# A two-layer trunk with seven-product MLPs: where the steps on the first two hidden panels stand ahead of each chunk's second matrix

## The chip, the cores and the metric

The kernel runs on one core of a Trainium2 chip. The metric is the device time of one execution in microseconds (us); the time of a kernel is the median of several runs. A profile is one execution, recorded by the hardware, with its own time.

## The reference

The input is x with 256 rows (tokens) of 2048 numbers in fp32. Two layers are applied. Each has an attention (the first a forgetting attention with its own keys and values, the second a chunked attention over shared keys and values) and then an MLP. Only the MLPs matter here:

```
def sq_relu_mlp(h, g, w1, w2):
    a = jax.nn.relu(rms_norm(h, g) @ w1)
    return (a * a) @ w2

h = h + sq_relu_mlp(h, mlp_norm_g[layer], mlp_w1[layer], mlp_w2[layer])
```

w1 is 2048 x 8192 and w2 8192 x 2048, for each of the two layers.

## The kernel before

**Products in three passes.** Each fp32 operand is split in two: a high part rounded to fp32r, made on ScalarE (line 217 for weights), and a low part, the difference, made on VectorE (line 218). A product is then three passes on TensorE: high by high (line 461), activation low by weight high (463), activation high by weight low (465). The name hi (hih for a half) is a weight's high part, lo (loh) its low part.

**Chunks, panels and pairs.** The hidden width of 8192 is worked in four chunks of 2048. A chunk takes four panels of 512 hidden columns of w1 (panels 0 to 3 of the chunk) and then four panels of 512 output columns of w2, whose input is the chunk's 2048 hidden values, that is 16 tiles of 128. Two panels make a pair (class `Pair`); a chunk is thus two pairs of the first matrix and two of the second, in this order. The 256 tokens are two blocks of 128.

**Seven products instead of eight.** For some of the 16 input tiles a pair uses a scheme of Strassen's kind: over two token blocks, two groups of tiles and two panels it takes seven block products ("forms", in the order 11, T3, T2, T1, 21, T4, 22) of sums of weights and sums of activations instead of eight. In a wide pair six of the 16 input tiles go this way, and each form has a full part (f0 to f6, tiles in two sets of two, 6 matmuls) and a half part (h0 to h6, 3 matmuls). The other ten tiles are plain products in units of two tiles (12 matmuls): a3 to a7 for the first panel of the pair, b3 to b7 for the second. In `form_products`, f0 reads the first four activation tiles of the chunk's hidden panel 0, and h0 reads tiles 4 and 5, which belong to panel 1; f1 to f3 and f6 read sums of panel 0's tiles, h1 to h3 and h6 sums of panel 1's. All pairs of w2 are wide, and all of w1 but the first of each layer.

**The order of the work** is written out by hand in `Pair.plan` (lines 131 to 142) and kept on VectorE, ScalarE, TensorE and the SP queue by `keep_order`. From the second pair of a chunk to its third pair (the first of w2) TensorE does

```
... f2 h2 b7 f3 h3 a3 f4 h4 a4 f5 h5 a5 f6 h6 a6 a7 b3 b4 | f0 h0 b5 f1 h1 b6 f2 h2 b7 ...
```

where the bar marks the start of the next pair; b5 to b7 behind it still belong to the pair before. The weight splits run ahead of the products: `fetch` and `top_up` (230 to 238) split up to three full weight tiles and one half tile ahead, and issue the loads of raw tiles from the SP queue (line 200, four buffers). The four corner tiles of a pair's forms are loaded by `bring` (line 800, SP queue), their sums made by `make` (line 810, VectorE) or by an accumulating load by `put` (line 816, POOL queue), each so many units before the pair starts (`prepare`): the corner 11 four units before, T3 three, T1 two, 21 one.

**The small steps** between the units come from a list, `fill`: after the products of each a or b unit (not after forms) `run_fill` issues the next entry. When a panel of w1 is done, `turn_hidden` (852) transposes it in 32 x 32 blocks on VectorE (line 329), and puts on the list: its store to memory (339) for the next unit, its load back with rows and columns exchanged (345) for the one after, and then the steps of `take` (828) by the numbers in `uses`, where n is the panel in the chunk, c the chunk, and a number i means the i-th a or b unit from then. The steps are: 1. ReLU on ScalarE (829); 2. square as the high part, ScalarE (834); 3. square in fp32 in place, ScalarE (836); 4. the low part, the difference, on VectorE (840); then for panels 0 and 1: 5. the sums and differences over the token blocks, four operations on VectorE (284 to 287, `sums`); 6. their high part on ScalarE (291); 7. their low part on VectorE (294). Panels 0 and 2 end with a7, panels 1 and 3 with the b7 that follows among the next pair's forms.

Of the kernel before, what the change touches and what calls it, by code (L numbers as in the profile page):

```python
# [49 lines left out]
def trunk(ctx: ExitStack, tc: tile.TileContext, xT, xr, gs, hg, bf, wgate, w_in, w_oa, w1a, w1fa, w1sa, w2fa, w2sa,  # L50
# [185 lines left out]
    def fetch(ahead=AHEAD, early=EARLY):  # L236
        top_up(ahead, early)
        return ready.popleft()[:2]
# [3 lines left out]
    def run_fill():  # L242
        if fill:
            for f in fill.popleft():
                f()
# [7 lines left out]
    def acc_pair(which=None):  # L253
        if which is None:
            which, turns[0] = turns[0], 1 - turns[0]
        if which == 2:
            return [ps_s.tile([P, 512], F32, name="s") for _ in range(2)]
        return [ps_acc.tile([P, 512], F32, name="acc", tag=f"acc{which}{b}", bufs=1) for b in range(NB)]
# [16 lines left out]
    def sums(a, fs, n=2):  # L275

        w = [wk.tile([P, 512], F32, name="sum", tag="wk") for _ in range(n)]

        def part(i):
            at = i * n * P  # L280
            v = w[at // 512][:, at % 512 : at % 512 + n * P].rearrange("p (g t) -> p g t", g=n)
            return v.rearrange("p g (i c) -> p g i c", i=4) if len(a[0][0].shape) == 4 else v

        V.tensor_tensor(part(0), a[1][0], a[1][1], op=ALU.subtract)
        V.tensor_tensor(part(1), a[0][0], part(0), op=ALU.subtract)
        V.tensor_tensor(part(2), a[1][0], a[0][0], op=ALU.subtract)
        V.tensor_tensor(part(3), a[0][1], part(1), op=ALU.subtract)
        hi, lo = ([fs[k][:, i * 512 : (i + 1) * 512] for i in range(n)] for k in range(2))
        yield
        for i in range(n):  # L290
            S.activation(hi[i], w[i], AF.Copy)
        yield
        for i in range(n):
            V.tensor_tensor(lo[i], w[i], hi[i].bitcast(F32), op=ALU.subtract)
        yield
# [21 lines left out]
    def steps(make):  # L317
        box = []

        def step():  # L320
            if not box:
                box.append(make())
            next(box[0])
        return step

    def blocks32(src, z, b):
        n = src.shape[1] // P
        nb = z.shape[1] // (n * P)
        V.transpose(z.rearrange("p (j n b c) -> p b n j c", j=4, n=n, b=nb)[:, b],
                    src.rearrange("p (n j c) -> p n j c", n=n, j=4))  # L330

    def carry(z, dst, wait=1):
        w = z.shape[1]
        n = w // 4
        box = []

        def rows():
            box.append(dram.tile([P, w], F32, name="turn", tag=f"turn{w}", bufs=4))
            SY.dma_start(box[0], z)

        def columns():
            s = box[0].rearrange("(i a) f -> a i f", i=4)
            d = dst.rearrange("p (i f) -> p i f", i=4)
            for j in range(4):
                SY.dma_start(d[32 * j : 32 * j + 32], s[:, :, j * n : (j + 1) * n])

        return [[rows]] + [[]] * wait + [[columns], [], []]

    def turned(name=None):
        z = qkv.tile([P, GH * T], F32, name="z")  # L350
        return (z, qkv.tile([P, GH * T], F32, name=name, tag=name, bufs=2)) if name else z
# [310 lines left out]
    def add_fill(items):  # L662
        for i, it in enumerate(items):
            if i < len(fill):
                fill[i] = fill[i] + it
            else:
                fill.append(it)
# [155 lines left out]
    def mlp(plan, x, Sx, st, last):  # L823
        base = turns[0]
        hids = [[] for _ in range(NCH)]
        Sh = [[] for _ in range(NCH)]

        def take(t, c, n):
            S.activation(t, t, AF.Relu)
            y = acts.tile([P, 2, GH, T], F32R, name="act")  # L830
            hi, lo = (y[:, i].rearrange("p k (b i c) -> p (k b) i c", b=NB, i=4) for i in range(2))
            t3 = t.rearrange("p (i kb c) -> p kb i c", i=4, c=32)
            yield
            S.activation(hi, t3, AF.Square)
            yield
            S.activation(t, t, AF.Square)
            yield

            def low():
                V.tensor_tensor(lo, t3, hi.bitcast(F32), op=ALU.subtract)  # L840

            hids[c].extend(y[:, :, j, :] for j in range(GH))
            low()
            yield
            if n == 0:
                r = prob.tile([P, 9 * 3 * P], F32R, name="Sh", tag="p", bufs=1)
                Sh[c].extend(r[:, i : i + n] for i, n in ((0, UN), (UN, UN), (2 * UN, 512), (2 * UN + 512, 512)))
                yield from sums([[t3[:, 2 * j + b :: 4] for j in range(2)] for b in range(NB)], Sh[c])
            elif n == 1:
                yield from sums([[t3[:, 2 * j + b : 2 * j + b + 1] for j in range(2)] for b in range(NB)], Sh[c][2:], 1)  # L850

        def turn_hidden(c, n):
            zt = []

            def f(b, ps):
                if b == 0:
                    zt.extend(turned("q"))
                blocks32(ps, zt[0], b)
                if b == NB - 1:
                    step = steps(lambda: take(zt[1], c, n))  # L860
                    uses = ((4, 5, 7, 8, 9, 10, 11), (4, 5, 6, 7, 7, 8, 8), (4, 5, 6, 7), (4, 5, 5, 5))[n]
                    if not c and n < 2:
                        uses = (4, 5, 6, 7, 7, 8, 8) if n else (4, 4, 5, 6, 7, 8, 9)
                    add_fill(carry(*zt, 0)[:2] + [[step] * uses.count(i) for i in range(3, uses[-1] + 1)])
            return f

        pairs = [p for p, q, u in plan if (q, u) == (2, 0)]

        def open_pair(p):
            m = pairs.index(p)  # L870
            c, second, r = m // 4, m % 4 >= 2, m % 2
            p.x, p.fs = (hids[c], Sh[c]) if second else (x, Sx)
            p.ps = [acc_pair(base), acc_pair(2 if p.third else 1 - base)]
            if second:
                p.evac = [(last if c == NCH - 1 else residual)(2 * r + q, st.r2) for q in range(2)]
            else:
                p.evac = [turn_hidden(c, 2 * r + q) for q in range(2)]

        starts = [i for i, it in enumerate(plan) if it[1:] == (2, 0)]
        for i, (p, q, u) in enumerate(plan):  # L880
            hi, lo = ready.popleft()[:2] if q > 1 and ready else fetch()
            if p.ps is None:
                open_pair(p)
            f, kind, k = plan[i - 1]
            done = k if i and kind > 1 and kind == 2 + f.wide else None
            if q > 1:
                form_products(p.ps, hi, lo, p.x, p.fs, u, q == 3, 1 + p.wide)
                if u == 1 and q == 2 + p.wide:
                    p.t["P7"] = wk.tile([P, 512], F32, name="p7", tag="wk")
                    S.activation(p.t["P7"], p.ps[1][0], AF.Copy)  # L890
                elif u == 2 and q == 2 + p.wide:
                    V.scalar_tensor_tensor(p.ps[0][1], p.ps[1][0], -1.0, p.t["P7"], op0=ALU.mult, op1=ALU.subtract)
                if q == 2 + p.wide:
                    top_up(AHEAD - 1)
                    if u == 1:
                        S.activation(p.ps[1][0], p.ps[1][1], AF.Copy, scale=-1.0)
            else:
                products(p.ps[q], hi, lo, p.x, u, not units and not ready, p.fast)
                if p.fast and (q, u) == (0, p.own):
                    V.tensor_tensor(p.ps[1][1], p.ps[1][0], p.t["P7"], op=ALU.add)  # L900
                run_fill()
                if u == KT // UA - 1:
                    for b in range(NB):
                        p.evac[q](b, p.ps[q][b])
                nxt = next((j for j in starts if j > i), None)
                if nxt is not None:
                    d = sum(1 for it in plan[i:nxt] if it[1] < 2)
                    prepare(plan[nxt][0], d)
            if done == 1 and not f.wide:
                make(f, "T4")  # L910
            elif done == 2:
                S.activation(f.ps[0][0], f.ps[1][1], AF.Copy)
# [144 lines left out]
```

## Time and profile before

| | |
|---|---|
| time, median of 3 runs | 2114.97 us (2114.54 to 2116.11) |
| time of the profiled execution | 2118.57 us |
| its span, first to last instruction | 2116.8 us |
| mean granted TensorE clock | 0.998 of full speed |
| busy, share of the span | TensorE weight loads 82%, VectorE 76%, ScalarE 59%, GpSimd 5% |
| moved by DMA | 538.85 MB, 255 GB/s in the mean |

The rows of the profile name an engine (PE is TensorE's products, PEld its weight loads, DVE VectorE, ACT ScalarE, POOL GpSimd, SPq the DMA issues of the SP queue), a line of the kernel, the operation, what is written and read, sizes and counts. In a timeline a row begins with its start and duration in us and ends, in brackets, with the idle time before it and what ended that. Ends of matmuls are modelled, so their rows overlap a little; start to start is the safer measure. In a list of waits the three numbers are the total in us, the times, and the longest.

### The profile page before, as it was taken

Reading aid. Unit: us, or ns where it says so; the run is one execution under the profiler, and the core shown is the slowest. Engines: PE = TensorE matmul, PEld = TensorE weight load, DVE = VectorE, ACT = ScalarE, POOL = GpSimd, SP = SyncE. Lnnn points to the kernel's source line nnn. Section 1 sums busy time; section 2 is a strip of 40 time slices with the busy share of each in tenths; the row PEclk is TensorE's granted clock in tenths of the full one; section 3 lists DMA queues with packets and bytes.
Section 4 is the critical chain, followed back from the end, with each engine's and each line's share of the span. In section 5 each row is a group of like instructions: output and inputs, shape, how many; then the busy total and the mean of one; then the engine's idle time right before and its main releaser. Section 6 shows DMA issues by size and latency. Waiting matters only on the chain.

```text
span 2116.8 us, 26314 instructions
## 1 busy us (share of the span) xinstructions
PE 2091.2 (99%) x9242; PEld 1727.1 (82%) x9242; DVE 1615.5 (76%) x1944; ACT 1247.8 (59%) x1623; POOL 109.9 (5%) x123
## 2 busy tenths in 40 slices
PE   9999999999999999999999999999999999999999
PEld 8888888878878887887888888888788788788877
DVE  5767666888788778778777677678877887888786
ACT  6544445676566566566675454456665665665664
POOL 1101000000000000000001010000000000000000
PEclk9999999999999999999999999999999999999999
DMA  7787788798797799789778777788888987987885
GB/s 282 245 258 241 232 248 262 259 267 267 249 285 241 249 288 274 215 277 283 229 237 263 233 233 234 237 273 261 273 254 251 278 265 238 282 258 244 276 270 169
DMA packets 181206, 538.85 MB, mean 255 GB/s; under 512 B 36800, under 2 KB 72016, under 8 KB 181072
## 3 DMA queue, kind: packets, MB, share of 16 engines
q1 hardware_dynamic: 171248, 484.69, 68.4%
q0 software_dynamic: 9824, 52.46, 13.5%
q8 instruction: 73, 1.20, 0.2%
q14 instruction: 61, 0.50, 0.1%
HBM read 497.20 MB, written 39.87 MB: 254 GB/s over the span
## 4 chain that ended last, share of the span: by engine, by line
PE 94%; DMA 3%; DVE 2%; issue 0%; SPq 0%; ACT 0%; DVEq 0%; ACTq 0%
PE acc L463 25%; PE acc L461 25%; PE acc L465 24%; PE s L463 6%; PE s L465 6%; PE s L461 6%; DVE lo L218 1%; DMA w<-in_w2fa 1%; PE s L604 1%; PE po L634 1%; DMA q<-turn 1%; DMA raw<-in_w2sb 0%; DMA w<-in_w2fb 0%; PE s L603 0%; PE po L635 0%
## 5 line engine op out<-in xcount | busy, mean ns | idle before, releaser
L218 DVE TENSOR_TENSOR lo<-raw,hi 128x1024 fp32r<-128x1024 f32 (+1 forms) x582 | 705.0, 1215 | 235.5 <-ACT hi L217 222.1
L217 ACT ACTIVATE hi<-raw 128x1024 fp32r<-128x1024 f32 (+1 forms) x582 | 611.5, 1052 | 288.3 <-PE acc L463 214.7
L461 PE MATMUL acc<-hi,act 128*128 128x512 f32 x2122 | 586.5, 395 | 0.7 <-ACT hi L217 0.5
L463 PE MATMUL acc<-hi,act 128*128 128x512 f32 x2122 | 578.2, 391 | 0.0
L465 PE MATMUL acc<-lo,act 128*128 128x512 f32 x2122 | 575.8, 390 | 0.0
L463 PEld LDWEIGHTS acc<-hi,act 128*128 128x128 f32 x2122 | 399.5, 189 | 86.6 <-DVE act L840 2.8
L465 PEld LDWEIGHTS acc<-lo,act 128*128 128x128 f32 x2122 | 399.4, 188 | 83.5
L461 PEld LDWEIGHTS acc<-hi,act 128*128 128x128 f32 x2122 | 397.5, 188 | 82.1 <-ACT hi L217 0.8
L217 ACT ACTIVATE hi<-w 128x1024 fp32r<-128x1024 f32 x130 | 137.3, 1056 | 97.4 <-DMA w<-in_w1fa 24.0
L218 DVE TENSOR_TENSOR lo<-w,hi 128x1024 fp32r<-128x1024 f32 x130 | 157.8, 1214 | 33.7 <-ACT hi L217 33.5
L218 DVE TENSOR_TENSOR lo<-wT,hi 128x1024 fp32r<-128x1024 f32 x94 | 114.6, 1219 | 75.4 <-ACT hi L217 74.2
L217 ACT ACTIVATE hih<-w 128x512 fp32r<-128x512 f32 x120 | 75.2, 627 | 74.3 <-PE acc L463 63.3
L217 ACT ACTIVATE hi<-wT 128x1024 fp32r<-128x1024 f32 x94 | 99.1, 1055 | 31.8 <-PE acc L463 17.5
L217 ACT ACTIVATE hih<-wT 128x512 fp32r<-128x512 f32 x90 | 56.5, 628 | 95.7 <-PE acc L463 63.3
L461 PE MATMUL s<-hi,act 128*128 128x512 f32 x392 | 106.2, 389 | 0.0
L463 PE MATMUL s<-hi,act 128*128 128x512 f32 x392 | 106.1, 389 | 0.0
L465 PE MATMUL s<-lo,act 128*128 128x512 f32 x392 | 106.1, 389 | 0.0
L218 DVE TENSOR_TENSOR loh<-w,hih 128x512 fp32r<-128x512 f32 x120 | 82.3, 686 | 22.0 <-ACT hih L217 22.0
L463 PEld LDWEIGHTS s<-hi,act 128*128 128x128 f32 x392 | 73.6, 188 | 15.3
L465 PEld LDWEIGHTS s<-lo,act 128*128 128x128 f32 x392 | 73.6, 188 | 15.3
L461 PEld LDWEIGHTS s<-hi,act 128*128 128x128 f32 x392 | 73.5, 188 | 15.2
L218 DVE TENSOR_TENSOR loh<-wT,hih 128x512 fp32r<-128x512 f32 x90 | 61.9, 688 | 19.4 <-ACT hih L217 19.4
(213 smaller groups left out, 1902.8 us busy)
## 6 DMA issues: line engine op xcount, KB each, us to landing
raw<-in_w_in SPq DMA_DIRECT2D x96, 512.0 KB, 4.6
raw<-in_w2sa SPq DMA_DIRECT2D x80, 512.0 KB, 5.7
raw<-in_w2sb SPq DMA_DIRECT2D x80, 512.0 KB, 5.6
raw<-in_w1sa SPq DMA_DIRECT2D x70, 512.0 KB, 6.0
raw<-in_w1sb SPq DMA_DIRECT2D x70, 512.0 KB, 6.0
raw<-in_w_kv SPq DMA_DIRECT2D x64, 512.0 KB, 4.5
turn<-z SPq DMA_DIRECT2D x60, 512.0 KB, 4.8
w<-in_w2fa SPq DMA_DIRECT2D x32, 768.0 KB, 7.3
```

The costliest lines, as they stand in the source:

```text
L217: S.activation(hi[:, c], raw[:, c], AF.Copy)
L218: V.tensor_tensor(lo[:, c], raw[:, c], hi[:, c].bitcast(F32), op=ALU.subtract)
L461: TE.matmul(ps[:, cols], xh, cut(hi, j), start=first, stop=False, **kw)
L463: TE.matmul(ps[:, cols], xl, cut(hi, j), start=False, stop=False, **kw)
L465: TE.matmul(ps[:, cols], xh, cut(lo, j), start=False, stop=last, **kw)
L604: TE.matmul(s[:, P : 3 * P], q[:, a, P:T], k[:, a], start=True, stop=True)
L634: TE.matmul(po[:, :T], v[:, 0, a * P : (a + 1) * P], pT[:, :2], start=True, stop=False)
```

## The change

Only the numbers of `uses` for panels 0 and 1 are changed; those of panels 2 and 3 stay.

```
-                    uses = ((4, 5, 7, 8, 9, 10, 11), (4, 5, 6, 7, 7, 8, 8), (4, 5, 6, 7), (4, 5, 5, 5))[n]
+                    uses = ((4, 5, 6, 7, 8, 9, 10), (4, 4, 5, 6, 6, 7, 7), (4, 5, 6, 7), (4, 5, 5, 5))[n]
                     if not c and n < 2:
-                        uses = (4, 5, 6, 7, 7, 8, 8) if n else (4, 4, 5, 6, 7, 8, 9)
+                        uses = (4, 4, 5, 6, 6, 7, 7) if n else (4, 4, 5, 5, 6, 7, 8)
```

The units after which the steps are issued, before and after (b3 and b4 ahead of the bar, b5 behind it, that is after f0 and h0):

| step | panel 0 before | after | panel 1 before | after |
|---|---|---|---|---|
| 1 ReLU | b6 | b6 | a6 | a6 |
| 2 high part | b7 | b7 | a7 | a6 |
| 3 square | a4 | a3 | b3 | a7 |
| 4 low part | a5 | a4 | b4 | b3 |
| 5 sums | a6 | a5 | b4 | b3 |
| 6 sums' high part | a7 | a6 | b5 | b4 |
| 7 sums' low part | b3 | a7 | b5 | b4 |

In the first chunk of a layer, whose first pair has another order, panel 0's ReLU and high part both come after a3 and its square after a4, before and after the change; the other entries hold there too. In one unit's entry panel 0's steps are issued ahead of panel 1's, and all of them ahead of the transposes of a panel that ends with the unit (panel 2 at a7). The splits of weights that a unit fetches are issued ahead of its entry: at a6 that of b3, at a7 that of b4, at b3 that of f0, at b4 those of h0 and b5, after h0 that of f1, at b5 those of h1 and b6.

## The prediction, made before the changed kernel was run

> **What bounds the kernel now.** I read the page first, then the waits of the matmul engine, then a table of stretches, and last the timelines of one chunk engine by engine.
>
> ```profile
> PE 2091.2 (99%) x9242; PEld 1727.1 (82%) x9242; DVE 1615.5 (76%) x1944; ACT 1247.8 (59%) x1623; POOL 109.9 (5%) x123
> ```
>
> TensorE is busy 99% of the span, so time can only come out of places where it stands still or runs slowly. Its list of waits has two entries that matter:
>
> ```profile
> PE s L463 <- DVE act L840: 14.3, 8, 2.7
> PE s L463 <- DVE Sh L294: 5.7, 5, 1.1
> ```
>
> Both lie in the steps that the change moves. Eight times, once for each chunk in each layer, the second pass (L463) of the half product h0 of a chunk's first second-matrix pair waits for panel 1's low part (L840). Five times the second pass of the next half product, h1, waits for panel 1's sums (L294). The wait column gives 20.0 us, but not what follows a wait, so I cut out the stretch from the first matmul of f0 to the first matmul of f2 in all eight chunks. The columns are the stretch, its length, the busy time of PE, PEld, DVE, ACT and POOL, the granted clock, the DMA share and GB/s.
>
> ```profile
> 458.43:470.51 12.08, 10.16 (x44) 7.73 (x42) 9.60 (x13) 5.03 (x9) 0.00 (x0) 1.00 0.94 258
> 627.13:640.54 13.41, 11.44 (x43) 8.95 (x42) 10.73 (x15) 6.31 (x10) 0.00 (x0) 0.87 0.84 231
> 797.16:810.24 13.08, 10.11 (x44) 7.73 (x42) 10.61 (x15) 6.19 (x10) 0.00 (x0) 1.00 0.94 241
> 966.86:980.43 13.57, 10.13 (x44) 7.73 (x43) 11.10 (x15) 6.69 (x11) 0.00 (x0) 1.00 0.88 235
> 1508.35:1522.25 13.90, 11.22 (x43) 8.78 (x42) 11.44 (x16) 7.01 (x11) 0.00 (x0) 0.88 0.84 223
> 1678.87:1691.90 13.03, 10.12 (x43) 7.72 (x42) 10.56 (x14) 6.15 (x10) 0.00 (x0) 1.00 0.89 241
> 1848.52:1862.15 13.63, 11.46 (x43) 8.98 (x42) 10.94 (x15) 6.52 (x11) 0.00 (x0) 0.87 0.94 232
> 2018.76:2030.80 12.04, 10.11 (x44) 7.73 (x42) 9.56 (x13) 5.00 (x9) 0.00 (x0) 1.00 0.94 255
> 980.43:989.95 9.52, 9.52 (x44) 7.88 (x43) 9.36 (x12) 9.48 (x13) 0.86 (x1) 1.00 0.71 162
> ```
>
> The first eight rows add to 104.74 us. The ninth is the same 42 matmuls one step on (f2, h2, b7, f3, h3, a3 in place of f0, h0, b5, f1, h1, b6), without a wait: 9.52 us, or 0.227 us for a matmul. Eight times 9.52 is 76.16, so these stretches lose **28.58 us**. That is the most the change can bring. In three rows the clock is 0.87 or 0.88: 13.41 x 0.13, 13.90 x 0.12 and 13.63 x 0.13 make 5.2 us of the 28.58.
>
> **What the change moves, worked out on chunk 4 of layer one (f0 starts at 966.86).** Panel 1's low part and sums go from b4 to b3, its square from b3 to a7, its high part from a7 to a6, its sums' high and low from b5 to b4. Panel 0's steps from the square on go one unit up too. No instruction is added or removed; only places in the queues change. The waiting half product:
>
> ```profile
> 968.22 0.39 PE L461 MATMUL s<-hih,act 128*128 128x512 f32 x1
> 970.90 0.50 PE L463 MATMUL s<-hih,act 128*128 128x512 f32 x1 [2.29 <-DVE act L840]
> ```
>
> Pass one of h0 starts at 968.22, so pass two could start at 968.45 and pass three, which reads h0's own low part loh, at 968.67. Pass two started at 970.90. This is what VectorE did before it:
>
> ```profile
> 959.09 1.23 DVE L218 TENSOR_TENSOR lo<-raw,hi 128x1024 fp32r<-128x1024 f32 x1 [0.18 <-ACT hi L217]
> 961.16 1.31 DVE L329 STREAM_TRANSPOSE z<-acc 128x512 f32<-128x512 f32 x2 [0.85 <-PE acc L465]
> 962.40 1.72 DVE L810 TENSOR_TENSOR wT<-w,w 128x1536 f32<-128x1536 f32 x1
> 965.55 1.23 DVE L218 TENSOR_TENSOR lo<-w,hi 128x1024 fp32r<-128x1024 f32 x1 [1.43 <-ACT hi L217]
> 966.69 1.29 DVE L294 TENSOR_TENSOR Sh<-sum,Sh 128x512 fp32r<-128x512 f32 x2
> 967.89 0.68 DVE L218 TENSOR_TENSOR loh<-w,hih 128x512 fp32r<-128x512 f32 x1
> 968.50 1.22 DVE L218 TENSOR_TENSOR lo<-raw,hi 128x1024 fp32r<-128x1024 f32 x1
> 969.63 1.22 DVE L840 TENSOR_TENSOR act<-q,act 128x1024 fp32r<-128x1024 f32 x1
> 970.76 0.28 DVE L284 TENSOR_TENSOR sum<-q 128x128 f32<-128x128 f32 x1
> ```
>
> In order: weight low part of b4, two transposes of panel 2, the sum T3, low part of f0, panel 0's two sums' low parts, loh of h0, low part of b5, panel 1's low part L840, panel 1's sums. L840 ends at 970.85 and h0 goes on at 970.90. Afterwards the order is: b4, panel 0's L294 pair, transposes, T3, f0, L840, sums, loh, b5, panel 1's L294. So the half product will no longer wait for L840 but, in pass three, for loh, behind which L840 and the sums now stand. How late loh comes decides the gain.
>
> *ScalarE first*, since it gates the split of b4:
>
> ```profile
> 955.04 1.06 ACT L217 ACTIVATE hi<-raw 128x1024 fp32r<-128x1024 f32 x1 [0.75 <-PE acc L463]
> 956.46 1.06 ACT L829 ACTIVATE q<-q 128x1024 f32<-128x1024 f32 x1 [0.35 <-DMA q<-turn]
> 957.99 1.06 ACT L217 ACTIVATE hi<-raw 128x1024 fp32r<-128x1024 f32 x1 [0.47 <-PE acc L463]
> 958.96 1.13 ACT L291 ACTIVATE Sh<-sum 128x512 fp32r<-128x512 f32 x2
> 960.00 1.04 ACT L834 ACTIVATE act<-q 128x1024 fp32r<-128x1024 f32 x1
> ```
>
> At a6 it now does after b3's high part (955.04, next start 0.97 later) panel 0's L291 pair (1.04 from start to start), L829 (whose data landed at 956.46) and panel 1's L834, about 1.0 each, and then b4's high part: 955.04 + 0.97 + 1.04 + 2.0 = 959.05 instead of 957.99. TensorE needs b4 one unit, 12 x 0.227 us, before f0, at 964.14, which covers the 1.06 us. VectorE's split of b4 follows 1.10 later, at 960.15 (1.14 to the next), the L294 pair at 961.29 (1.20), the transposes at 962.49 (1.24), T3 at 963.73 (1.72), and VectorE is free for f0 at 965.45.
>
> *Whether f0 is there* depends on its load, w<-in_w2fa, which the ScalarE and SP queues show:
>
> ```profile
> 964.45 1.06 ACT L217 ACTIVATE hi<-w 128x1024 fp32r<-128x1024 f32 x1 [3.41 <-DMA w<-in_w2fa]
> ```
>
> ```profile
> 954.06 2.60 SPq L200 DMA_DIRECT2D raw<-in_w1sa  x2
> 956.71 0.42 SPq L800 DMA_DIRECT2D w<-in_w2fa  x1
> ```
>
> The load of form "11" is issued at 956.71, right behind the second of two raw loads, and that one waits for a raw buffer, which the weight low part of a7 on VectorE frees. Ahead of that split stand now panel 0's four sums instead of its low part:
>
> ```profile
> 953.95 1.22 DVE L840 TENSOR_TENSOR act<-q,act 128x1024 fp32r<-128x1024 f32 x1
> 955.08 2.36 DVE L218 TENSOR_TENSOR lo<-raw,hi 128x1024 fp32r<-128x1024 f32 x2
> 957.36 0.42 DVE L284 TENSOR_TENSOR sum<-q 128x256 f32<-128x256 f32 x1
> ```
>
> The sums took 957.36 to 958.91 (959.09 less the 0.18 of idle time), 1.55 us; L840 takes 1.13. The split slips by 0.42 and the load with it. f0's high part starts at 964.87, its low part 1.10 later (964.45 to 965.55 before), at 965.97, a little after VectorE is free.
>
> *Then* L840 at +1.14, sums at +2.27, loh at +3.20 (970.76 and the next row give 0.94 for the sums), done 0.68 later; with 0.05 for the semaphore pass three starts 3.94 after f0's low part, at 969.91:
>
> ```profile
> 971.70 1.22 DVE L218 TENSOR_TENSOR lo<-wT,hi 128x1024 fp32r<-128x1024 f32 x1
> ```
>
> That is 1.24 us after 968.67, where the stretch lost 4.05. **The second gap goes:** h1 starts at 974.2 with f1 and b5 in between. VectorE then does b5 (969.78), panel 1's L294 (970.9), f1 (971.5), loh of h1 (972.6, done at 973.3); h1 wants its sums at 974.4 and its loh at 974.7; f1 wants its low part, done at 972.7, at 973.8. Margins are 1.0 us or more, so I cost it at nothing; without them it would be the 1.1 us of the old wait.
>
> *The other chunks* differ only in when "11" lands. The latest and earliest of the eight rows:
>
> ```profile
> 1506.32 1.06 ACT L217 ACTIVATE hi<-w 128x1024 fp32r<-128x1024 f32 x1 [3.79 <-DMA w<-in_w2fb]
> ```
>
> ```profile
> 2014.62 1.06 ACT L217 ACTIVATE hi<-w 128x1024 fp32r<-128x1024 f32 x1 [1.68 <-DMA w<-in_w2fb]
> ```
>
> With 1.52 added, f0's low part starts 0.51 before f0 in the one and would start 2.62 before in the other; there VectorE's own chain rules (965.45 is 1.41 before 966.86). The gap is that start plus 3.94 less 1.81: 1.62 us at most, 0.72 at least. By the same sum the eight gaps are 0.72, 0.91, 0.77, 1.24, 1.62, 0.72, 1.12 and 0.72, together 7.8 us. The slow clock goes with the long gaps: the two shortest stretches, 12.08 and 12.04, have 1.00.
>
> *What I cost at nothing.* Panel 0's low part at a4 and its square at a3: between them and a5 lie T4's products and a whole unit of TensorE work; if that cover were gone, up to 1.13 us would be added to the slip of the load in each chunk. SP: the store of the transposed panel 2 waits for the transposes, 1.33 us later (961.16 to 962.49), and behind it in the queue stand a raw load for a unit beyond f3, the four column loads and the load of "21", which f4 is first to use. The tightest reader is panel 2's ReLU:
>
> ```profile
> 966.89 2.60 SPq L345 DMA_DIRECT2D q<-turn  x4
> ```
>
> ```profile
> 981.29 1.05 ACT L829 ACTIVATE q<-q 128x1024 f32<-128x1024 f32 x1
> ```
>
> Issue ends at 969.49, the reader starts 11.8 us later. The change takes 1.33 and the 2.8 gained by TensorE from that and leaves 7.7, as long as the six times larger load "11" takes from 956.71 to its reader at 964.45. POOL: the accumulating load of T1 waits for T3 and slips by 1.3 as well; its form is split for f3 only, whose products follow those of f2 (980.43 less the 2.8 gained).
>
> **The sum.** 28.6 less 7.8 is 20.8 us. The profiled execution took 2118.57 us by its own time, so 2097.8 in its terms. It was 3.6 us above the median of the three timed runs, and 2114.97 less 20.8 is **2094.2 us**.
>
> **One rule weighed.** The Trainium skill, page "TensorE: Matmul & The Clock Gate", section "What's actually happening", says that the array falls to half its clock after at least one idle activity window of about 3.4 us, on a window that does not start with the kernel. Here no wait is that long (the longest in the waits view is 2.7 us), and yet three stretches show 0.87 or 0.88: the trace does not agree with the figure. By that rule alone the slow clock would have another cause and stay, which is the second rival.
>
> **The rivals.**
> 1. *VectorE slips further.* Its chain from b4 to loh is 9.7 us of work in order with one late start (ScalarE's 959.05). If L291, L829 or L834 wait, everything behind slips, and the gap grows one for one: 1 us in each chunk makes 8 us, a gain of 12.8, 2102.2 us. Against it: L829's data was there at 956.46, and the sums that L291 reads end at 955.5, before 956.01.
> 2. *The slow clock stays* in three chunks, as it would if the gaps were not its cause: 5.2 us less gain, 2099.4. Against it: 1.00 in the ninth row and in the short ones.
> 3. *Nothing left to wait for:* loh comes in time, 28.6 us, 2086.4. It would need VectorE 0.7 to 1.6 us faster than its rows.
> 4. *No change:* the place in the list is changed but the wait is only renamed, loh taking the place of L840. This needs f0's low part 2.6 us later on average than worked out (20.8 / 8).
> 5. *Slower:* the load of "11". Every us by which its issue slips behind 957.1 moves f0's high part, and in-order VectorE with it, one for one in eight places. It decides from a slip of 0.42 + (20.8 + 4.2) / 8 = 3.5 us on; at 4.5 us the kernel takes 2114.97 + 4.2 + 8 x 1.0, about 2127. The rows give only 0.42 and at worst 1.13 more.
>
> **How the numbers follow.** About 0.2%, 4.2 us, is what a measurement of this kernel can tell from no change. The forecast gets 0.70, rival 1 0.10, rival 2 0.07, rival 3 0.03, rival 4 0.06, rival 5 0.04. Faster: the first four, 0.90; same 0.06; slower 0.04. The range runs from rival 3's 2086.4 to 2102, where each gap is twice what I work out or rival 1 has its 1 us; it takes in rival 2 and leaves out half of rival 1 and the last two, some 0.15, and a little of the forecast.
>
> **What would show it.** In the changed profile: no wait of h0 for L840 and none of h1 for L294; eight waits for loh (L218) at L465 of 0.7 to 1.6 us; the eight stretches at 10.2 to 11.2 us with the clock at 1.00; the transposes 1.3 us later; b4's high part 1 us later; the load of "11" 0.4 us later. Wrong it would be if h0 waits for more than 2 us, or if a wait for DMA appears at panel 2's ReLU.

## The result and the profile after

The changed kernel takes **2096.22 us** (median of 4 runs, 2095.46 to 2097.20), the kernel before beside it 2115.39 us (4 runs, 2114.54 to 2116.11). The ratio is 0.991, with a 95% interval of 0.9893 to 0.9927: 19.2 us faster, where 20.8 were forecast and 2094.2 us was the predicted time.

The profiled execution of the changed kernel took 2095.46 us, with a span of 2093.7 us. First, as before, the busy times of the page, and the top of the matmul engine's list of waits:

```profile
PE 2084.1 (100%) x9242; PEld 1722.6 (82%) x9242; DVE 1614.2 (77%) x1944; ACT 1247.8 (60%) x1623; POOL 110.0 (5%) x123
```

```profile
PE s L465 <- DVE loh L218: 3.9, 8, 0.5
```

The waits for L840 (14.3 us) and L294 (5.7 us) are gone from the list. One name is new, the one forecast: pass three (L465) of h0 waits for loh, eight times, 0.5 us each. The table of stretches from f0 to f2, in the columns of the prediction's table, and last the stretch without a wait:

```profile
457.36:467.68 10.32, 9.83 (x43) 7.80 (x42) 9.69 (x13) 5.57 (x9) 0.00 (x0) 1.00 1.01 245
624.32:634.62 10.30, 9.81 (x43) 7.81 (x42) 9.68 (x13) 5.57 (x9) 0.00 (x0) 1.00 1.01 251
791.24:801.58 10.34, 9.85 (x43) 7.80 (x42) 9.68 (x13) 5.57 (x9) 0.00 (x0) 1.00 1.01 234
958.22:968.56 10.34, 9.85 (x43) 7.80 (x42) 9.68 (x13) 5.57 (x9) 0.00 (x0) 1.00 1.01 244
1496.49:1506.81 10.32, 9.83 (x43) 7.80 (x42) 9.69 (x13) 5.57 (x9) 0.00 (x0) 1.00 1.00 201
1663.45:1673.75 10.30, 9.81 (x43) 7.80 (x42) 9.68 (x13) 5.57 (x9) 0.00 (x0) 1.00 1.01 225
1830.37:1840.72 10.35, 9.86 (x43) 7.81 (x42) 9.69 (x13) 5.57 (x9) 0.00 (x0) 1.00 1.00 219
1997.38:2007.69 10.31, 9.82 (x44) 7.80 (x42) 9.69 (x13) 5.57 (x9) 0.00 (x0) 1.00 0.99 226
968.56:978.08 9.52, 9.52 (x43) 7.88 (x42) 9.37 (x12) 9.52 (x13) 0.86 (x1) 1.00 0.97 267
```

All eight lengths lie between 10.30 and 10.35 us and the clock is 1.00 in each. They add to 82.58 us; less 8 x 9.52 this is **6.4 us lost**, against 28.6 before. The difference, 22.2 us, is nearly all of the 23.1 us between the two profiled executions. Another 1.07 us lie ahead of the first chunk, whose f0 starts at 457.36 instead of 458.43.

Chunk 4 of layer one, on TensorE:

```profile
959.58 0.39 PE L461 MATMUL s<-hih,act 128*128 128x512 f32 x1
959.80 0.39 PE L463 MATMUL s<-hih,act 128*128 128x512 f32 x1
960.68 0.50 PE L465 MATMUL s<-loh,act 128*128 128x512 f32 x1 [0.49 <-DVE loh L218]
961.02 1.11 PE L461 MATMUL acc<-hi,act 128*128 128x512 f32 x4
961.97 1.08 PE L463 MATMUL acc<-hi,act 128*128 128x512 f32 x4
```

Pass two of h0 follows pass one without a pause. Pass three could have started at 960.03 and starts at 960.68, 0.65 us late. A little more is lost right behind: this matmul and the next are 0.34 us apart where 0.227 us is the rule, and the four matmuls that follow take 0.95 us (961.02 to 961.97) where four take 0.91. That makes 0.15 us, and 0.80 us with the 0.65; the eight chunks lose 0.80 us in the mean. VectorE in the same chunk:

```profile
951.52 1.23 DVE L218 TENSOR_TENSOR lo<-raw,hi 128x1024 fp32r<-128x1024 f32 x1 [2.40 <-ACT hi L217]
952.67 1.29 DVE L294 TENSOR_TENSOR Sh<-sum,Sh 128x512 fp32r<-128x512 f32 x2
953.87 1.31 DVE L329 STREAM_TRANSPOSE z<-acc 128x512 f32<-128x512 f32 x2
955.10 1.72 DVE L810 TENSOR_TENSOR wT<-w,w 128x1536 f32<-128x1536 f32 x1
956.74 1.21 DVE L218 TENSOR_TENSOR lo<-w,hi 128x1024 fp32r<-128x1024 f32 x1
957.87 1.22 DVE L840 TENSOR_TENSOR act<-q,act 128x1024 fp32r<-128x1024 f32 x1
959.00 0.29 DVE L284 TENSOR_TENSOR sum<-q 128x128 f32<-128x128 f32 x1
...
959.94 0.68 DVE L218 TENSOR_TENSOR loh<-w,hih 128x512 fp32r<-128x512 f32 x1
960.54 1.22 DVE L218 TENSOR_TENSOR lo<-raw,hi 128x1024 fp32r<-128x1024 f32 x1
961.68 0.68 DVE L294 TENSOR_TENSOR Sh<-sum,Sh 128x512 fp32r<-128x512 f32 x1
```

This is the order that the prediction wrote down: b4, panel 0's L294 pair, the transposes, T3, f0, L840, the sums, loh, b5, panel 1's L294. From 952.67 on no row waits for anything: the low part of f0 starts as soon as VectorE is free, 1.48 us before f0 (958.22). ScalarE, and the load of form "11" on the SP queue:

```profile
949.48 1.06 ACT L834 ACTIVATE act<-q 128x1024 fp32r<-128x1024 f32 x1
950.45 1.04 ACT L217 ACTIVATE hi<-raw 128x1024 fp32r<-128x1024 f32 x1
...
953.84 1.06 ACT L217 ACTIVATE hi<-w 128x1024 fp32r<-128x1024 f32 x1 [1.40 <-DMA w<-in_w2fa]
```

```profile
945.42 2.93 SPq L200 DMA_DIRECT2D raw<-in_w1sa  x2
948.40 0.42 SPq L800 DMA_DIRECT2D w<-in_w2fa  x1
```

The high part of b4 (950.45) stands behind panel 1's L834. It starts 7.77 us before f0 (8.87 before the change) and gates VectorE's 951.52, as forecast. The load is issued 9.82 us before f0 (10.15 before the change). Its data is there at 953.84, 5.44 us after the issue; before the change the same interval was 7.74 us (956.71 to 964.45).

### The profile page after: what moved, and what is told of

It is laid out like the page before. It is cut to its first block, busy times and chain, and to the rows that moved or that the text cites. A ratio compares the mean times of both kernels' runs of the same rounds, so it can differ in the third digit from the quotient of the medians.

```text
span 2093.7 us, 26322 instructions
## 1 busy us (share of the span) xinstructions
PE 2084.1 (100%) x9242; PEld 1722.6 (82%) x9242; DVE 1614.2 (77%) x1944; ACT 1247.8 (60%) x1623; POOL 110.0 (5%) x123
## 3 DMA queue, kind: packets, MB, share of 16 engines
q0 software_dynamic: 9824, 52.46, 13.7%
## 4 chain that ended last, share of the span: by engine, by line
PE 99%; DVE 0%; DMA 0%; SPq 0%; issue 0%; ACT 0%; DVEq 0%
PE acc L463 26%; PE acc L461 26%; PE acc L465 26%; PE s L465 6%; PE s L461 6%; PE s L463 6%; PE s L604 1%; PE po L634 1%; PE s L603 0%; PE po L635 0%; DVE loh L218 0%; DMA raw<-in_w_in 0%; PE s L726 0%; DVE sum L287 0%; DVE lo L218 0%
## 5 line engine op out<-in xcount | busy, mean ns | idle before, releaser
L465 PE MATMUL acc<-lo,act 128*128 128x512 f32 x2122 | 574.5, 389 | 0.0
L465 PEld LDWEIGHTS acc<-lo,act 128*128 128x128 f32 x2122 | 398.1, 188 | 83.1
L465 PE MATMUL s<-lo,act 128*128 128x512 f32 x392 | 106.1, 389 | 0.0
L465 PEld LDWEIGHTS s<-lo,act 128*128 128x128 f32 x392 | 73.6, 188 | 15.3
```

The costliest lines, as they stand in the source:

```text
L465: TE.matmul(ps[:, cols], xh, cut(lo, j), start=False, stop=last, **kw)
```

## The experiments

All twelve profiles of this study can be read with one table. For each, the eight stretches from f0 to f2 were measured as above, and 8 x 9.52 us taken off:

| kernel | profiled execution, us | lost in the eight stretches, us | difference, us |
|---|---|---|---|
| before | 2118.57 | 28.58 | 2089.99 |
| before, again | 2113.68 | 24.46 | 2089.22 |
| before, low part twice | 2128.13 | 39.22 | 2088.91 |
| before, load sooner | 2109.21 | 20.20 | 2089.01 |
| panel 0's new places only | 2108.33 | 19.43 | 2088.90 |
| panel 1's new places only | 2097.44 | 8.57 | 2088.87 |
| after | 2095.46 | 6.42 | 2089.04 |
| after, again | 2095.64 | 6.58 | 2089.06 |
| after, low part twice | 2110.15 | 19.96 | 2090.19 |
| high part back | 2090.70 | 1.59 | 2089.11 |
| high part back, again | 2091.75 | 2.73 | 2089.02 |
| high part back, load sooner | 2090.21 | 0.32 | 2089.89 |

The last column lies within 0.3 us of 2089 in nine of the twelve. The three that stand 0.9 to 1.2 above it have their first f0 at 458.24 to 458.49 us instead of 457.2 to 457.6, so their extra lies ahead of the first chunk. But for this, what these kernels differ in is lost in the eight stretches. Theory A in the texts below is the prediction's mechanism: VectorE's order sets how soon h0's operands come, and the load of "11" adds to it where it lands late.

**One panel at a time.** The change moves the steps of two panels. The first kernel takes only panel 1's new numbers, the second only panel 0's:

```
-uses = ((4, 5, 6, 7, 8, 9, 10), (4, 4, 5, 6, 6, 7, 7), ...)[n]
+uses = ((4, 5, 7, 8, 9, 10, 11), (4, 4, 5, 6, 6, 7, 7), ...)[n]    # e1; first chunk likewise
+uses = ((4, 5, 6, 7, 8, 9, 10), (4, 5, 6, 7, 7, 8, 8), ...)[n]     # e2; first chunk likewise
```

> Only panel 1's numbers are changed, panel 0's stay as before. VectorE's order at the end is then: b4, transposes of panel 2 (old place), T3, f0, panel 0's L294 pair, L840, panel 1's sums, loh. Theory A (h0 now waits for loh, and loh comes when everything ahead of it in VectorE's order is done): the L294 pair, 1.20 us, is back between f0 and loh, so a gap is S + 3.33, with S the start of f0's low part against f0 on TensorE. If the load of form 11 takes as long as before the change (5.9 to 8.1 us from issue to reader), S goes from -2.75 to -0.93 and the eight stretches lose about 13 us, some 2103 us in all. If the load takes as long as after the change (5.4 to 6.5 us), S is -2.75 everywhere and they lose about 6 us, 2096 us. Theory B (h0 waits for panel 1's own chain only, so panel 0's steps do not matter): the same time as after the change, 2096 us, with the same wait of 0.65 us.

> Only panel 0's numbers are changed, panel 1's stay as before. L840 of panel 1 stands again behind loh and b5, and its sums' low part behind b6. Theory A: h0 waits in pass two for L840, S + 2.56, that is 0.2 us with the fast load and up to 2.0 with the slow one; h1 waits 1.1 to 1.4 us for L294 in every chunk. Loss 15 us with the fast load and 23 with the slow one: 2105 to 2113 us. Theory B: panel 0's part brings nothing, 2115 us.

Panel 1 alone: 2099.41 us (2097.01 to 2103.30), ratio to before 0.993 (0.9918 to 0.9943), 15.6 us faster. Panel 0 alone: 2108.41 us (2106.75 to 2112.97), ratio 0.9972 (0.9963 to 0.9981), 6.6 us faster. The first lies between the two times that theory A gave for it, the second inside its range; theory B's 2096 and 2115 us did not come. The matmul engine's waits, panel 1 alone and then panel 0 alone:

```profile
PE s L465 <- DVE loh L218: 5.4, 8, 1.0
```

```profile
PE s L463 <- DVE Sh L294: 7.9, 7, 1.1
PE s L463 <- DVE act L840: 5.5, 4, 2.6
```

Panel 1's move does the main part: it turns the waits for L840 and L294 into the wait for loh. Panel 0's move leaves both, but takes its own L294 pair off VectorE ahead of L840, so that only four waits for L840 are left. In the first kernel the wait is not the same in each chunk. Its stretches lose from 0.65 to 1.80 us, and they follow the start of f0's low part: where that is 2.82 us before f0, 0.66 us are lost, where it is 1.67 us before f0, 1.80. Theory A's sum for this order, the start plus 3.33 us, gives 0.51 and 1.66, and with the 0.15 us behind a pause both losses. The load behind these two took 6.19 and 7.38 us from its issue to its reader. So the load has a part in the wait, chunk by chunk, as theory A has it.

**The high part back at its old place.** The prediction found that panel 1's high part (L834) at a6 stands ahead of b4's high part on ScalarE and makes all of VectorE 1 us late. This kernel is the changed one with that single step back at a7:

```
-(4, 4, 5, 6, 6, 7, 7)
+(4, 5, 5, 6, 6, 7, 7)      # panel 1, in all chunks
```

> The changed kernel, with panel 1's high part (L834) back at a7, so that b4's high part on ScalarE stands 0.96 us earlier. Theory A: VectorE's whole chain from b4 on starts 0.96 us earlier, transposes at about -5.3 against f0 instead of -4.35, and if f0's load lands as after the change, S is about -2.4 and loh is there in time: no wait of h0, the eight stretches at about 9.6 us, 6 us faster than the changed kernel, 2090 us. Theory C (the load of form 11 lands 1 to 2 us earlier after the change because the store of panel 2 and the raw load behind it now come later): with the transposes earlier the load is slow again, S from -2.4 to -0.6, gaps from 0 to 1.5 us, sum 6 us, and the time stays at 2096 us.

It takes 2091.35 us (2089.43 to 2092.37), ratio to before 0.9891 (0.9877 to 0.9904): 23.6 us faster, 4.4 more than the whole change. Two stretches of its table, and its one entry for h0:

```profile
955.77:966.14 10.37, 9.81 (x43) 7.80 (x42) 9.76 (x13) 5.60 (x10) 0.00 (x0) 1.00 0.98 257
789.59:799.11 9.52, 9.52 (x44) 7.88 (x42) 8.65 (x12) 5.58 (x9) 0.00 (x0) 1.00 0.96 213
```

```profile
PE s L465 <- DVE loh L218: 1.0, 2, 0.6
```

In the second of these stretches b4's high part stands ahead of L834 again, and f0's low part starts 2.51 us before f0:

```profile
780.77 1.06 ACT L217 ACTIVATE hi<-raw 128x1024 fp32r<-128x1024 f32 x1
781.74 1.04 ACT L834 ACTIVATE act<-q 128x1024 fp32r<-128x1024 f32 x1
```

```profile
787.08 1.21 DVE L218 TENSOR_TENSOR lo<-w,hi 128x1024 fp32r<-128x1024 f32 x1
```

Six of the eight stretches take 9.52 us, the length without any wait. In them f0's low part starts 2.43 to 2.51 us before f0, one us sooner than in the changed kernel. In the other two it starts 1.41 and 1.52 us before f0, with loads of 7.31 and 7.20 us, and 0.85 and 0.75 us are lost. The changed kernel loses 0.80 us with a start of 1.48 us: both lie on one line, *lost = start of f0's low part relative to f0, plus 2.27 us, if positive*. Theory C, that panel 2's store slows the load when it runs beside it, isn't borne out: the transposes are back at 5.38 us before f0 here, and the loads take 5.33 to 7.31 us; at 5.69 us in the kernel with panel 1's places only they take 5.6 to 7.4, and at 4.35 in the changed kernel 5.4 to 6.5 us in one profile and 5.3 to 7.5 in another. Over all profiles, the 24 loads with the transposes at about 5.4 us took 6.2 us in the mean, and the 24 with them at about 4.35 us 6.2 as well. The time stayed 5 us below the 2096 us that theory C gave.

**The low part twice.** To see whether VectorE's order prices the stretch one for one, panel 1's low part is made twice, in the changed kernel and in the kernel before. The second operation writes the same values again.

```
             low()
+            if n == 1:
+                low()
```

> The changed kernel, with panel 1's low part made twice in a row (the second writes the same values over the first), which adds 1.13 us on VectorE ahead of the sums and loh in each chunk. Theory A: loh comes 1.13 us later, the wait of h0 at L465 grows from 0.65 to 1.8 us in all eight chunks, 9 us in all: 2105 us. Rival (ScalarE or the load of form 11 sets the gap, VectorE has slack): less than 3 us.

> The kernel before, with panel 1's low part made twice in a row, which lengthens each of the eight waits of h0 by 1.13 us, to between 1.9 and 3.9 us. If long gaps bring the slow clock (theory A), the five or six stretches whose gap passes 2.3 us run at a granted clock of 0.87 and lose 1.7 us more each: 2115.4 + 9 + 5 to 8 us, 2130 us, and the shortest two keep 1.00. If the slow clock has nothing to do with the gaps (rival 2 of the prediction), about as many slow stretches as before and 2124 us.

The changed kernel with it takes 2106.55 us (2105.28 to 2111.11), 10.3 us more than without. h0 in chunk 4 now waits twice:

```profile
967.49 0.39 PE L461 MATMUL s<-hih,act 128*128 128x512 f32 x1
968.32 0.50 PE L463 MATMUL s<-hih,act 128*128 128x512 f32 x1 [0.44 <-DVE act L840]
969.85 0.50 PE L465 MATMUL s<-loh,act 128*128 128x512 f32 x1 [1.03 <-DVE loh L218]
```

Six stretches lose 2.04 to 2.08 us, that is 1.25 more than in the changed kernel. This is the repeated operation alone: from the start of L840 to the first sum VectorE now takes 2.39 us instead of 1.13, so the second one costs 1.26 us and not the 1.13 us that the expectation had. The price is one for one. Two pay more: one with a load of 7.73 us loses 2.59, and the first loses 5.06, with its load issued 1.6 us later and the clock at 0.88. Of these 5.06 us the slow clock takes 1.6: the standing still of TensorE and the 0.15 us behind it make 3.4.

The kernel before with it takes 2127.57 us (2125.02 to 2128.13), ratio 1.0062 (1.0047 to 1.0077), 13.75 us more, between the two expectations. The pause of h0 itself shows theory A's price: where f0's low part starts 2.82 us before f0, it is 2.20 us here and 0.94 us in the kernel before, again 1.26 us. All eight pauses are now 2.0 us or longer, and TensorE is slow after each, also in the stretches that the expectation had at a clock of 1.00. Chunk 4, after a wait of 3.27 us:

```profile
973.25 0.80 PE L463 MATMUL s<-hih,act 128*128 128x512 f32 x1 [3.27 <-DVE act L840]
973.84 0.63 PE L465 MATMUL s<-loh,act 128*128 128x512 f32 x1
974.27 1.91 PE L461 MATMUL acc<-hi,act 128*128 128x512 f32 x4
975.97 1.42 PE L463 MATMUL acc<-hi,act 128*128 128x512 f32 x4
977.23 1.09 PE L465 MATMUL acc<-lo,act 128*128 128x512 f32 x4
...
979.75 0.39 PE L463 MATMUL s<-hih,Sh 128*128 128x512 f32 x1
```

The first two passes of b5 take 2.96 us (974.27 to 977.23) where 1.81 is normal. But the pass of h1 at 979.75, which waits for L294 in the kernel before, finds its sums ready: the slow matmuls have used up that wait. Beyond the pause itself, this stretch loses 1.74 us. The stretches of the kernel before at a clock of 1.00 lose 1.55 to 1.62 us beyond their pause, most of it (1.3 us) in the wait of h1. So a slow clock costs that kernel some 0.15 us net for a stretch. One of the eight stretches here pays more, 2.9 us beyond its pause: its clock stayed low for 6.8 us instead of 3.4 (the length 15.97 us, the clock 0.79).

**Before once more, and where its spread comes from.** The 17 runs of the kernel before beside the first experiments lie between 2112.15 and 2117.84 us, and its first profile was 3.6 us above the median. The same kernel again:

> The kernel before, unchanged, to see how the number of stretches with a clock under 1.00 differs from one execution to the next. The profiled execution had three, 5.2 us, at 2118.57 us; that makes 2113.4 us with none. If each costs 1.7 us, timed runs at 2114.5 to 2116.1 have one or two, and the gain of 20.8 us worked out from the profiled execution is 2 to 4 us too large for the timed runs. If the three always come, the profile should show the same three and about 2115 us.

2115.27 us (2110.06 to 2116.44), ratio 1.0002 (0.9992 to 1.0011). The profiled execution took 2113.68 us and lost 24.46 us in the eight stretches, with the clock below 1.00 in one of them, the first of these two:

```profile
1504.96:1518.51 13.55, 11.43 (x43) 8.95 (x42) 10.89 (x15) 6.47 (x10) 0.00 (x0) 0.87 0.88 228
1675.12:1688.50 13.38, 10.20 (x44) 7.73 (x42) 10.90 (x15) 6.48 (x10) 0.00 (x0) 1.00 0.82 231
```

The two rows have nearly the same load (7.56 and 7.52 us) and nearly the same wait for L840 (2.12 and 2.08 us); the clock falls in one and not in the other (the last section shows why), and the lengths differ by 0.17 us. A price of 1.7 us for each slow stretch, with which I had reckoned, is wrong. What differs between the two profiles is the load: 6.00 to 8.12 us in the first, 5.34 to 7.56 in the second. The next kernel tests that. It is the kernel before with the load of "11" one unit sooner for the first pair of the second matrix:

```
-                add(None, w2f, w2s, i, WIDE2, "wide", close)
+                add(None, w2f, w2s, i, WIDE2, "wide", close if q else (7, 5, 1, 5, 3, 2))
```

> The kernel before, with only the load of form 11 issued one unit sooner in the same eight places. Theory A (the spread of the eight gaps, 2.5 to 4.4 us of loss, comes from the landing of that load, and so do the stretches with a slow clock): S is -2.8 in all eight, each stretch loses 2.5 us, 20.2 in all, the clock is 1.00 throughout; against the second profile of the kernel before (24.5 us lost, one slow stretch) that is 4.3 us less, 2109 to 2110 us. Rival (the load is hidden, the gaps are VectorE's order alone): 2114 us.

It takes 2109.43 us, and its 11 runs lie between 2109.09 and 2110.45: ratio 0.9979 (0.9970 to 0.9988). The load is now issued 14.28 us before f0 instead of 10.15. The eight stretches lose 2.51 to 2.56 us, all at a clock of 1.00:

```profile
457.38:469.41 12.03, 10.10 (x43) 7.73 (x42) 9.56 (x13) 4.99 (x9) 0.00 (x0) 1.00 0.94 254
```

```profile
PE s L463 <- DVE Sh L294: 9.2, 8, 1.1
PE s L463 <- DVE act L840: 6.2, 8, 0.8
```

Both waits of the kernel before are there, each at its smallest. So the late landing of "11" gave the kernel before its spread, its slow clock and 4.6 us of its median (2114.02 beside these runs). The rest, 20.2 us, is VectorE's order, which is what the change treats.

**The best version.** Both together, the high part back at a7 and the load one unit sooner:

> The changed kernel with panel 1's high part back at a7, and with the load of form 11 of each chunk's first second-matrix pair issued five units ahead instead of four, about 16 us before f0 instead of 9.8. Theory A (what is left is set by VectorE's chain or, where it lands late, by that load): the load lands 8 us before f0 at the latest, S is -2.4 to -2.5 in all eight chunks and none of them waits: 9.52 us each, 1.5 to 3 us faster than with the high part back alone, 2089 us. Rival (earlier, the load only takes bandwidth or a buffer from the raw tiles that TensorE needs next): a new wait for DMA in the units a5 to b3, and no gain, 2091 to 2095 us.

> The changed kernel once more, beside the others on one chip. Eight waits of h0 for loh; VectorE's own chain sets them to 0.65 us where the load of form 11 is issued and lands within 7.2 us, so at least 6.4 us of loss, more in executions where it takes longer: 2095.5 to 2098 us.

> The changed kernel with panel 1's high part back at a7 once more, for an interval against the changed kernel on the same chip: 4 to 6 us faster than it, 2091 us.

The combination takes **2089.20 us** (2088.88 to 2090.21), ratio to before 0.9884 (0.9871 to 0.9898). On the same chip the changed kernel took 2095.72 us (2095.22 to 2095.89; 0.9914, 0.9901 to 0.9928) and the one with the high part back 2091.60 us (2089.77 to 2093.40; 0.9895, 0.9881 to 0.9908). Two of the eight stretches of the combination:

```profile
458.24:468.08 9.84, 9.81 (x44) 7.81 (x42) 9.22 (x13) 5.58 (x9) 0.00 (x0) 1.00 1.01 239
624.74:634.26 9.52, 9.52 (x44) 7.88 (x42) 8.65 (x12) 5.57 (x9) 0.00 (x0) 1.00 0.92 232
```

The load is issued 14.28 us before f0 in seven stretches, not the 16 us that were expected. These seven take 9.52 us. The first has its load issued 2 us later than the others, starts f0's low part 1.94 us before f0 and loses 0.32: the line above gives 2.27 - 1.94 = 0.33. That is not because this load landed late: f0's high part starts at 453.00 without a wait for it. At 436.92 ScalarE had waited 2.87 us for panel 0's transposed data (2.76 us in the first chunk of the changed kernel with its low part twice), which may be what delayed this chunk; no run isolates it. The high part back alone loses 1.77 us in the chunk with a load of 8.19 us and a start of 0.54, for which the line gives 1.73. Of the 28.6 us that the kernel before lost, next to nothing is left.

Beside these runs the change itself gains 18.3 us (2114.02 to 2095.72). By the kernel before with its load sooner, an estimate is that 4.6 us of this are late landings that no longer set the time, and 13.7 us VectorE's order.

## Why the prediction was right, and where its sum was off

*The chain of VectorE:* right. The order, the wait that takes the place of the others (pass three, for loh) and its size at VectorE's own pace were forecast at a start of f0's low part 1.41 us before f0 and a gap of 0.72 us; measured are 1.48 and 0.65. The high part of b4 was to slip by 1.06 us against f0 and slipped by 1.10, the transposes by 1.33 and 1.35, the load of "11" by 0.42 and 0.33.

*The second gap:* gone in all eight chunks, as forecast. *The slow clock:* gone with the long gaps (rival 2 falls), and back in all eight stretches of the kernel before when its pauses were made longer. A long gap alone does not bring it, though: it also depends on where the gap lies in time (last section). And the 5.2 us that the prediction read in the three slow stretches were never there to be had by themselves: without the slow clock they would have lost nearly as much in the wait of h1.

*The terms that were mis-sized.* First, the landing of "11". I took each chunk's time from issue to reader from the one profile of before, 6.0 to 8.1 us, and let it set the gaps of five chunks (0.77 to 1.62 us where the floor is 0.72). After the change the loads took 5.4 to 6.5 us in the profile, and none of the eight starts depends on them. That is 2.1 us too much; 8 x 0.07 us of the floor goes the same way, and 8 x 0.15 us for the slower matmuls behind a pause, which I had not counted, the other: 7.82 - 2.06 - 0.56 + 1.20 gives 6.40, the measured loss. These numbers aren't a property of a chunk at all: the same kernel showed others in its next profile (7.54 us for chunk 4 of the changed kernel, where the first profile has 5.44).

Second, the base. 28.6 us is what one dear execution lost. The table says that time is 2089 us plus the loss, so the median of 2115.39 stands for a loss of about 26.4, and 2096.22 for 7.2: 19.2 us. I took a gain measured on an execution 3.6 us above the median off the median itself. The base alone was 2.6 us too low (2114.97 less 28.6 is 2086.4, not 2089), the loss of 7.8 was 0.6 above the 7.2 of the median. These errors, of opposite sign, left the time 2.0 us too low; that it came so near is in part luck.

*The cost that the prediction saw and priced, but did not question:* b4's high part behind L834. It says that the slip is covered by a unit of TensorE work, and so it was for b4; but the same slip passes on to f0, L840 and loh, and there it is the whole of the remaining gap wherever the load of "11" lands in time. The high part back at a7 shows it by itself: 4.1 us between two medians taken on one chip.

*The rivals.* Rival 1 (VectorE 1 us later) and rival 3 (nothing left) did not come; what rival 3 says, with its base put right 2089 instead of 2086.4, is what the best version reaches, by the other order of ScalarE and the sooner load. Rival 4 had the right name, a renamed wait, at less than a fifth of the 3.6 us that it needed (0.98 on average and 2.6 more). Rival 5 (the load) needed a slip of 3.5 us and got 0.33; the load's spread is real, but it hurt the kernel before more than the one after, whose VectorE is later than the load.

*What stays open* is why the load of "11" takes 5.3 to 8.4 us in the same place from one execution to the next. Panel 2's store was one candidate and the runs speak against it. Where panel 0's steps are at their old places, 32 loads took 6.8 us in the mean, against 6.2 us in the 48 others with the load at its old place; no run isolates what in panel 0's steps would do that. The other transfers that run beside it were not tried.

## What to carry to other kernels

When a step is moved sooner to clear one wait, write out what it now stands in front of on its own engine: one of the moves here, panel 1's high part from a7 to a6, put 1 us in front of the split that everything behind depends on, and undoing it gained more than a fifth on top of the whole change. Take the size of a wait from what is in order on an engine where that is the later side, and treat the landing of a load as a spread, not as a number of that chunk. A gain that is read from one execution is to be set against that execution's own time, or against several profiles, since a kernel whose waits hang on a load differs by several us from run to run.

## What the runs showed of the hardware

The clock falls after shorter pauses than I had supposed, and the length of a pause alone does not decide it. Over all profiles the stretch showed a clock of 0.79 to 0.89 after waits of h0 of 1.97, 2.04, 2.12, 2.17, 2.18, 2.54 us and longer, and 1.00 after 2.08 and 2.29 us and after every single wait up to 1.83 us. With one matmul between two waits of 1.43 and 1.03 us (the first chunk of the changed kernel with its low part twice) it fell as well.

The moments at which it falls show what does decide. In the kernel before, the granted clock falls to 0.50 at 631.74, 1512.38 and 1853.71 us; the distances are 258 and 100 times 3.4133 us. In the kernel before with its low part twice it falls at 461.25, 631.92, 802.58, 973.25, 1515.97, 1686.64, 1860.71 and 2031.38 us, that is after 50, 50, 50, 159, 50, 51 and 50 times 3.413 us. It stays at 0.50 for 3.41 us each time, once for twice that. So it is set anew every 3.41 us, on a grid that runs on through the kernel. Here are four windows of this grid in the kernel before: two around the fall at 631.74, and the two over which the wait of 2.29 us in chunk 4 is spread. The columns are the window, its length, PE's busy time, the clock, the DMA share and GB/s.

```profile
628.33:631.74 3.41, 1.44 (x7) 1.00 1.00 226
631.74:635.15 3.41, 3.41 (x10) 0.50 1.10 289
966.25:969.66 3.41, 2.36 (x11) 1.00 1.05 205
969.66:973.07 3.41, 2.17 (x9) 1.00 1.08 227
```

The first window holds 1.97 us in which TensorE stands still, and the next one runs at 0.50. The last two hold 1.05 and 1.24 us, and the clock stays: the wait of 2.29 us is longer, but the grid cuts it in two. Along the grids of all twelve profiles there are some 7300 windows at full clock. Each of the 22 with 1.97 us or more of standing still (14 in the stretches, 8 at the kernel's end) was followed by a fall, and none of those with 1.77 us or less; between these two values there was no window.

The Trainium skill, page "TensorE: Matmul & The Clock Gate", section "What's actually happening", gives an idle window of about 3.4 us that runs on its own. The traces agree with its length (3.413 us) and with its running on its own; they do not agree that the whole window has to be idle, since 1.97 us of it were enough. The prediction held the window's length against its longest wait, 2.7 us, and took the figure for contradicted; the length was right.

One transfer of 768 KB, issued at the same place of the same program, reached its reader after 5.3 us in one chunk and after 8.4 us in another (both in the profile with panel 0's new places only). And a slow clock is not simply lost time: in the kernel before it fell nearly whole on the wait that would have followed, and the stretch grew by 0.15 us. Where no such wait follows, as in the first chunk of the changed kernel with its low part twice, it cost 1.6 us.
